# A decoder layer's down projection: order of the weight sums, place of the spare load buffers, and ten split places in the second half

## The chip, the cores and the metric

The kernel runs on one core of a Trainium2 chip. The metric is the device time of one execution in microseconds (us), the median of several runs. A core has five engines with one instruction queue each: PE (matrix products), DVE and POOL (elementwise), ACT (elementwise and functions) and SP (here: it issues DMA transfers). PE writes into eight banks of its accumulator memory; the other engines and the DMA work on the on-chip memory of 128 partitions.

## The reference, cut to what matters

The layer is attention and then a gated feed-forward with a causal depthwise convolution; all is float32, for 256 tokens, a width of 2048 and an inner width of 5632. The change lies in the last product of the feed-forward, here called the down projection:

```python
h = rmsnorm(x, pre_ffn_g)
u = causal_dwconv(h @ w_up, conv_w, conv_b)          # (256, 11264)
gate, val = jnp.split(u, 2, axis=-1)
y = (gelu(gate) * val) @ w_down                      # (256, 5632) @ (5632, 2048)
out = x + rmsnorm(y, post_ffn_g)
```

## The kernel before, in words

**Splitting.** Each float32 operand of a product is split into a high part (ACT copies it into a rounded format, line 333) and a low part (DVE subtracts the high part from the original, line 334); both are in `split` (L332). A product is then three matmuls: high by high, high by low, low by high (`product`, L989).

**Two halves.** The inner width is worked through in two halves (`half`, L1075). Each half computes 11 groups of 256 inner channels with `proj_T4`, `conv` and the gate, and keeps them, split, in the tiles `G` (22 of them) and `sums`. Then come two column passes over `w_down` (n = 0 and n = 2, L1181), each for 1024 of the 2048 output columns. A group is one unit `u` of a pass: two blocks of 128 rows of `w_down`, 1024 columns wide.

**Plain and fast units.** `FAST` holds the units 0, 2, 4, 5, 6 and 7. The other five are plain: two loads, two splits, and eight products (two blocks, two halves of the tokens, two halves of the columns). A fast unit is a 2x2 block product done with seven products (a Winograd scheme): `token_sums` has made the sums of the token side, and the weight side needs three loads. `b11` is 512 columns of the first block. `r13` (1024 columns) is a difference that was formed in DRAM before (`pair_sums`). `r2` (1024 columns) is the second block. `f13` and `b2` are the splits of `r13` and `r2`. Two additions on DVE (L1019 and L1020) then form two more sums, in place in `r2`'s buffer, and `f24` is their split. The seven products take b11 once and each of b2, f13 and f24 twice, in the order of `steps` (L1034). The first fast unit of a pass has an order of its own (L1039).

**The order of units** (L1177 to L1179). Pass n = 0, in both halves: 1, 3, 0, 2, 4, 8, 5, 6, 7, 9, 10. Pass n = 2: 0, 2, 1, 4, 5, 3, 6, 7, 8, 9, 10 in the first half, and 0, 2, 4, 1, 5, 6, 7, 3, 8, 9, 10 in the second. The last unit of a pass is held back (its weights are split but not used at once), and its products are done bank by bank at the end (`block`, L1066), so that each bank can be read out while the next is finished. In the second pass of the second half the last three units are held (`HOLD` is 3): six split forms, which each of the four last blocks reads.

**Load buffers.** `load` (L1132) takes the next of a cycle of buffers of 512 KB: five of the tile `raw`, then `extra`, then two in the room that the convolution's outputs had (`spare`, tag `gates`), and in the second half two more in the room of `hT` (`more`), the input of the up projection. So the cycle has 8 buffers in the first half and 10 in the second. The transfer is issued on SP.

**Split places.** `parts` (L1141) takes the next of a cycle of 6 places for a high and a low part: five of the tiles `whi` and `wlo`, and one pair, `slots`, in the room that the convolution's inputs had (tag `room`). A place is free again when the last product that reads it is done. Each pass makes 34 splits (two per plain unit, four per fast one) and 28 loads (two and three); a half makes 68 and 56.

**Order on the engines.** On PE the program order is kept. On the other engines a planner with a cost model of its own orders the instructions when the kernel is built: an instruction is placed when the planner takes it to be ready, the earlier in the program first. From L1222 on, the order of ACT, DVE, POOL and SP is also that of the program.

**The end** (L1222 to L1262). `x_back` (the residual) and `gbf` (the gain `post_ffn_g`, copied to all partitions, 1 MB) are loaded on SP. `gbf` is a tile with the tag `hT`, so it lies in the first 2048 columns of `hT`'s room. POOL multiplies finished parts of `y` with `gbf` (`gain`, L1196); in its queue the order is `gain` four times, the power that gives the first 128 tokens' factor (`rstd_y`, L1211), `gain` four more times, the power for the other tokens, and a last `gain`. DVE adds the last blocks to `y` (`down`, L1117) and does the final step (`finish`, L1217); the two `finish` steps of the first tokens stand in its queue ahead of `down` of the third block. SP and ACT send the results out.

Of the kernel before, what the change touches and what calls it, by code (L numbers as in the profile page):

```python
# [8 lines left out]
F32 = mybir.dt.float32  # L9
F32R = mybir.dt.float32r  # L10
BF16 = mybir.dt.bfloat16
AF = mybir.ActivationFunctionType
ALU = mybir.AluOpType
# [4 lines left out]
P = 128  # L18
# [14 lines left out]
def hybrid_layer(ctx: ExitStack, tc: tile.TileContext, x, pre_mix_g, w_in, b_forget, sinks,  # L33
# [3 lines left out]
    pe, act, dve, pool, sp = nc.tensor, nc.scalar, nc.vector, nc.gpsimd, nc.sync  # L37
    xf, of = x[0], out[0]
# [4 lines left out]
    main = ctx.enter_context(tc.tile_pool(name="main", bufs=1))  # L43
# [6 lines left out]
    def bank(tag="acc"):  # L50
        return ps.tile([P, 512], F32, tag=tag, bufs=4, name="bank_" + tag)
# [13 lines left out]
    UNIT = 1024  # L65
# [32 lines left out]
    def w_parts(n, keep=None, still=False):  # L98


        if keep and keep[0] is None:
            return keep[1]
        if keep:
            return [keep[0].tile([P, UNIT], F32R, tag="h" + x, bufs=keep[1], name="w" + x)[:, :n]
                    for x in ("hi", "lo")]
        hi = wp.tile([P, UNIT], F32R, tag="whi", bufs=WB, name="whi")
        lo = wp.tile([P, UNIT + 128], F32R, tag="wlo", bufs=WB, name="wlo")
        c = LOW if still else 0
        return [hi[:, :n], lo[:, c:c + n]]
# [31 lines left out]
    def w_unit(src, a, c, keep=None):  # L141
        return w_split(w_load(src, a, c), keep=keep)

    def w_rows(w, k0, a, c0, c):
        return w[k0 * P:(k0 + a) * P, c0:c0 + c].rearrange("(a p) c -> p a c", p=P)
# [61 lines left out]
    hT = main.tile([P, KT, 512], F32R, tag="hT", name="hT")  # L207
# [124 lines left out]
    def split(hi, lo, src):  # L332
        act.copy(hi, src)  # L333
        dve.tensor_tensor(lo, src, hi.bitcast(F32), op=ALU.subtract)  # L334

    with tc.tile_pool(name="mixp", bufs=1) as mp:
# [54 lines left out]
        for u in range(4):  # L391
            if u:
                parts = w_split(first[0][u], True, still=True)
            else:
                parts = w_split(first[0][u], True, begun=begun,
                                between=lambda: x_part(0, (1,), "acc"))
# [5 lines left out]
            parts = w_split(first[1][u], True, still=True)  # L402
# [238 lines left out]
        for g in range(4):  # L641
            if g == 0:
                b2 = bq0
            else:
                b2 = [bank(), bank()]
# [6 lines left out]
        for p0, npair, cols in ((0, 3, 384), (3, 3, 384), (6, 2, 272)):  # L652
            b2 = [bank(), bank()]
            c0 = 3328 + p0 * P
            per = 3 if cols == 272 else 2
            for k0 in range(0, KT, per):
                na = min(per, KT - k0)
                hi, lo = w_unit(w_rows(w_in, k0, na, c0, cols), na, cols)
# [106 lines left out]
        hT = hT2  # L765
# [56 lines left out]
        for n in (2, 3):  # L822
            for u in range(4):
                raw = w_load(w_rows(w_out, 8 + u * 2, 2, n * 512, 512), 2, 512)
# [22 lines left out]
        turns = [turn(0, 0), turn(0, 1)]  # L847
# [8 lines left out]
        turns = [turn(0, 2), turn(0, 3)]  # L856
# [11 lines left out]
    with tc.tile_pool(name="ffn", bufs=1) as fp:  # L868
# [120 lines left out]
        def product(b, lh, ll, rhs, cols, first, last, to=None):  # L989
            hi, lo = rhs  # L990
            for i, (a, r) in enumerate(((lh, hi), (lh, lo), (ll, hi))):
                pe.matmul(b[:, to] if to else b, a, r[:, cols], start=(first and i == 0),  # L992
                          stop=(last and i == 2))

        def column_pass(G, sums, weights, some, order, k00, c0, load, parts, hold=1):

            left, right = slice(0, 512), slice(512, UNIT)
            fast = [u for u in order if u in some]
            plain = [u for u in order[:-hold] if u not in some]
            ready, started, held, banks = {}, set(), [], []  # L1000

            def of(k, t):
                return G[k][:, t * P:(t + 1) * P], G[k][:, 256 + t * P:256 + (t + 1) * P]

            def first(bk):
                new = id(bk) not in started
                started.add(id(bk))
                return new

            def prepare(u):  # L1010
                k = k00 + 2 * u
                if u not in some:
                    return [parts(load(w_rows(w_down, k + a, 1, c0, UNIT)), UNIT)
                            for a in range(2)]
                b11 = parts(load(w_rows(w_down, k, 1, c0, 512)), 512)
                r13 = load(weights[u][:, c0:c0 + UNIT].rearrange("p (a c) -> p a c", a=1))
                r2 = load(w_rows(w_down, k + 1, 1, c0, UNIT))
                f13, b2 = parts(r13, UNIT), parts(r2, UNIT)
                dve.tensor_tensor(r2[:, right], r2[:, right], r13[:, left], op=ALU.add)  # L1019
                dve.tensor_tensor(r2[:, left], r2[:, left], r2[:, right], op=ALU.add)  # L1020
                return b11, b2, f13, parts(r2, UNIT)

            def ahead():
                ready[order[0]] = prepare(order[0])

            def seven(u, forms, m1, m5, m7, m6, p2, p3, p4):
                k, end = 2 * u, u == fast[-1]
                b11, b2, f13, f24 = forms

                def s_of(j):  # L1030
                    return of(k, 1) if j == 3 else [sums[u][:, i * 384 + j * P:i * 384 + (j + 1) * P]
                                                    for i in range(2)]

                steps = [(m1, of(k, 0), b11, left), (p2, of(k + 1, 0), b2, left),  # L1034
                         (p3, s_of(2), b2, right), (m5, s_of(3), f13, left),
                         (m7, s_of(0), f13, right), (m6, s_of(1), f24, right),
                         (p4, of(k + 1, 1), f24, left)]
                if u == fast[0]:
                    steps = steps[0:1] + steps[3:] + steps[1:3]  # L1039
                for bk, a, b, cols in steps:  # L1040
                    product(bk, *a, b, cols, first(bk), end and bk in (m1, m5, m7, m6))

            def run(add_early):
                early, late = ([bank(tag) for _ in range(4)] for tag in ("acc", "att"))
                banks.extend(zip(late, (0, 0, 1, 1), (left, right, left, right)))
                for i, u in enumerate(order):
                    forms = ready.pop(u) if u in ready else prepare(u)
                    if u in some:
                        seven(u, forms, *early, *late[:3])
                        if u == fast[-1] and hold == 1:  # L1050
                            nxt = order[i + 1]
                            ready[nxt] = prepare(nxt)
                            add_early(*early)
                    elif i >= len(order) - hold:
                        held.extend((2 * u + a, forms[a]) for a in range(2))
                    else:
                        for a in range(2):
                            for bk, t, cols in banks:
                                product(bk, *of(2 * u + a, t), forms[a], cols, first(bk),
                                        hold > 1 and bk is late[3] and a == 1 and  # L1060
                                        u == plain[-1])
                if hold > 1:
                    add_early(*early)
                return late

            def block(i, bk=None, cols=None):  # L1066
                b, t, c = banks[i]
                for n, (k, w) in enumerate(held):
                    product(bk or b, *of(k, t), w, cols or c, bk is not None and n == 0,
                            n == len(held) - 1, cols and slice(cols.start - 512, cols.stop - 512))  # L1070

            return ahead, run, block

        ysq = [small.tile([P, 5], F32, tag=f"ysq{t}", bufs=1, name=f"ysq{t}") for t in range(2)]
        for half in range(2):  # L1075
# [5 lines left out]
            for g in range(FHALF // 2):  # L1081
# [25 lines left out]
                if g in FAST:  # L1107
                    i = FAST.index(g)
# [13 lines left out]

            slots = fp.tile([P, ROOM], F32R, tag="room", name="slots")
            slots = [slots[:, 32 + i * UNIT:32 + (i + 1) * UNIT] for i in range(2)]
            spare = fp.tile([P, 2, UNIT], F32, tag="gates", name="spare")
            raws, units = [fp.tile([P, UNIT], F32, tag="extra", name="extra")], [0, 0]
            raws += [spare[:, i, :] for i in range(2)]
            if half:
                more = main.tile([P, 2, UNIT], F32, tag="hT", name="more")
                raws += [more[:, i, :] for i in range(2)]  # L1130

            def load(src):  # L1132
                i = units[0] % (5 + len(raws)) - 5
                units[0] += 1
                c = src.shape[-1]
                if i < 0:
                    return w_load(src, 1, c)[0]
                sp.dma_start(raws[i][:, :c].rearrange("p (a c) -> p a c", a=1), src)
                return raws[i]

            def parts(src, n):  # L1141
                i = units[1] % 6 - 5
                units[1] += 1
                hi, lo = w_parts(n) if i < 0 else [x[:, :n] for x in slots]
                split(hi, lo, src[:, :n])
                return hi, lo

# [33 lines left out]
            for n, (_, run, block) in zip((0, 2), passes):  # L1181
# [6 lines left out]
                for i in range(4):  # L1188
                    block(i)
                    t, c = divmod(i, 2)  # L1190
# [48 lines left out]
        r = rstd_y(0, 3, v)  # L1239
# [18 lines left out]
        r = rstd_y(1, 4, v)  # L1258
        gain(1, 3, 1, last)
        for i, n in enumerate((512, 512, 512, 256, 256)):  # L1260
            c = (0, 512, 1024, 1536, 1792)[i]
# [30 lines left out]
```

## Time and profile before

| | |
|---|---|
| median of 3 runs | 1097.34 us (1096.88 to 1098.96) |
| the profiled execution's own time | 1100.12 us |
| its span, from first to last instruction | 1098.4 us |
| PE busy | 1062.6 us, 97% of the span |
| DVE busy | 855.5 us, 78% |
| ACT busy | 648.6 us, 59% |
| mean granted clock of PE | 0.983 |

The two passes of the first half begin at 581.5 us of the span, those of the second half at 953.1 us. A row of a timeline gives start and duration in us, engine, line, operation, what is written from what, the shape, the number of instructions in it, and in brackets how long the engine had been idle and what released it. In the name of a tile the buffer's number is left out. `SPq` is SP's issue of a transfer. A matmul's duration in a row includes its way through the array; in a row of back-to-back matmuls one starts every 0.23 us. "PEclk" is the clock that PE was granted, 1.00 being full speed.

### The profile page before, as it was taken

Reading aid. Unit: us, or ns where it says so; the run is one execution under the profiler, and the core shown is the slowest. Engines: PE = TensorE matmul, PEld = TensorE weight load, DVE = VectorE, ACT = ScalarE, POOL = GpSimd, SP = SyncE. Lnnn points to the kernel's source line nnn. Section 1 sums busy time; section 2 is a strip of 40 time slices with the busy share of each in tenths; the row PEclk is TensorE's granted clock in tenths of the full one; section 3 lists DMA queues with packets and bytes.
Section 4 is the critical chain, followed back from the end, with each engine's and each line's share of the span. In section 5 each row is a group of like instructions: output and inputs, shape, how many; then the busy total and the mean of one; then the engine's idle time right before and its main releaser. Section 6 shows DMA issues by size and latency. Waiting matters only on the chain.

```text
span 1098.4 us, 16433 instructions
## 1 busy us (share of the span) xinstructions
PE 1062.6 (97%) x5866; PEld 916.9 (83%) x5866; DVE 855.5 (78%) x1389; ACT 648.6 (59%) x1116; POOL 249.4 (23%) x280
## 2 busy tenths in 40 slices
PE   9999999999999999999998989999999999988986
PEld 7899988888889888888886768888888888866765
DVE  5988878876478888878875888867878887768985
ACT  6776757766466765656563545555556565545551
POOL 3254244440032231313130000012222222100013
PEclk9999999999999999999998989999999999989988
DMA  8748688765985987878775657778786866647562
GB/s 277 242 130 238 180 235 243 196 201 168 321 248 174 308 258 224 228 229 235 223 209 163 218 184 245 253 205 239 216 251 211 221 192 198 205 161 261 164 257 77
DMA packets 170798, 238.56 MB, mean 217 GB/s; under 512 B 7996, under 2 KB 132188, under 8 KB 169692
## 3 DMA queue, kind: packets, MB, share of 16 engines
q1 hardware_dynamic: 163184, 222.25, 62.9%
q0 software_dynamic: 6528, 12.58, 7.8%
q10 hardware_dynamic: 1004, 2.68, 0.6%
q8 instruction: 46, 0.75, 0.3%
q14 instruction: 36, 0.29, 0.1%
HBM read 233.14 MB, written 29.38 MB: 239 GB/s over the span
## 4 chain that ended last, share of the span: by engine, by line
PE 76%; DVE 11%; DMA 4%; issue 4%; ACT 4%; POOL 1%; DVEq 0%; SPq 0%; POOLq 0%; ACTq 0%
PE bank_acc L305 15%; PE bank_att L305 13%; PE bank_acc L330 9%; PE bank_acc L311 8%; PE bank_att L311 7%; PE bank_acc L274 7%; PE bank_att L992 7%; DVE wlo L334 4%; PE bank_acc L279 4%; PE bank_acc L992 2%; DVE slots L334 2%; ACT whi L333 1%; DMA spare<-in_w_down_dram 1%; DMA raw<-in_w_out_dram 1%; PE bank_att L496 1%
## 5 line engine op out<-in xcount | busy, mean ns | idle before, releaser
L136 DVE TENSOR_TENSOR wlo<-raw,whi 128x1024 fp32r<-128x1024 f32 (+3 forms) x271 | 332.8, 1241 | 110.5 <-ACT whi L133 102.8
L133 ACT CAST whi<-raw 128x1024 fp32r<-128x1024 f32 (+3 forms) x270 | 273.1, 1029 | 115.1 <-issue 63.4
L922 POOL TENSOR_TENSOR room<-room,rowf 128x256 f32<-128x256 f32 x88 | 100.4, 1160 | 367.5 <-DVE room L921 366.4
L305 PE MATMUL bank_acc<-hT,whi 128*128 128x512 f32 x736 | 173.3, 390 | 0.0
L305 PEld LDWEIGHTS bank_acc<-hT,whi 128*128 128x128 f32 x736 | 136.4, 188 | 27.4
L305 PE MATMUL bank_att<-hT,whi 128*128 128x512 f32 x640 | 150.6, 390 | 0.0
L305 PEld LDWEIGHTS bank_att<-hT,whi 128*128 128x128 f32 x640 | 118.7, 188 | 23.9
L992 PE MATMUL bank_att<-whi,G 128*128 128x512 f32 x342 | 117.6, 404 | 0.0
L924 ACT ACTIVATE room<-room,cw 128x256 f32<-128x256 f32 x88 | 53.0, 602 | 68.5 <-POOL room L922 68.5
L333 ACT CAST whi<-raw 128x1024 fp32r<-128x1024 f32 (+1 forms) x69 | 65.1, 973 | 46.2 <-DVE raw L1020 24.1
L334 DVE TENSOR_TENSOR wlo<-raw,whi 128x1024 fp32r<-128x1024 f32 (+1 forms) x69 | 76.7, 1139 | 19.7 <-ACT whi L333 19.7
L311 PEld LDWEIGHTS bank_acc<-hT,wlo 128*128 128x128 f32 x736 | 89.3, 188 | 2.0
L311 PE MATMUL bank_acc<-hT,wlo 128*128 128x256 f32 x736 | 89.9, 279 | 0.0
L274 PE MATMUL bank_acc<-hT,whi 128*128 128x512 f32 x352 | 88.0, 395 | 0.0
L330 PE MATMUL bank_acc<-whi,oT 128*128 128x512 f32 (+1 forms) x272 | 81.7, 379 | 0.0
L992 PEld LDWEIGHTS bank_att<-whi,G 128*128 128x128 f32 x342 | 67.6, 198 | 14.8
L311 PEld LDWEIGHTS bank_att<-hT,wlo 128*128 128x128 f32 x640 | 77.6, 188 | 1.7
L311 PE MATMUL bank_att<-hT,wlo 128*128 128x256 f32 x640 | 77.9, 279 | 0.0
L926 DVE SCALAR_TENSOR_TENSOR room<-room,cw 128x256 f32<-128x256 f32 x88 | 62.4, 709 | 17.6 <-ACT room L924 17.3
L274 PEld LDWEIGHTS bank_acc<-hT,whi 128*128 128x128 f32 x352 | 63.3, 188 | 11.6
L992 PE MATMUL bank_att<-wlo,G 128*128 128x512 f32 x171 | 69.5, 407 | 0.6 <-DVE wlo L334 0.6
L330 PEld LDWEIGHTS bank_acc<-whi,oT 128*128 128x128 f32 x272 | 50.2, 188 | 9.3
(263 smaller groups left out, 1704.6 us busy)
## 6 DMA issues: line engine op xcount, KB each, us to landing
raw<-in_w_up_dram SPq DMA_DIRECT2D x176, 512.0 KB, 4.6
raw<-in_w_in_dram SPq DMA_DIRECT2D x51, 512.0 KB, 5.6
raw<-in_w_down_dram SPq DMA_DIRECT2D x41, 512.0 KB, 4.8
raw<-in_w_out_dram SPq DMA_DIRECT2D x32, 512.0 KB, 5.8
t<-in_w_down_dram SPq DMA_DIRECT2D x24, 512.0 KB, 6.7
t<-in_w_down_dram POOLq DMA_DIRECT2D x24, 512.0 KB, 8.3
spare<-in_w_down_dram SPq DMA_DIRECT2D x15, 512.0 KB, 5.0
raw<-in_w_in_dram SPq DMA_DIRECT2D x16, 384.0 KB, 3.3
```

The source lines that it names most:

```text
L133: i1 = act.copy(hi[:, cs], raw[:, cs])
L136: i2 = dve.tensor_tensor(lo[:, cs], raw[:, cs], hi[:, cs].bitcast(F32), op=ALU.subtract)
L274: pe.matmul(b, parts[u][0][:, a, m * P:(m + 1) * P], hT[:, kt, :], start=(kt == 0), stop=(kt == KT - 1))
L305: pe.matmul(b, parts[u][0][:, a, m * P:(m + 1) * P], hT[:, kt, :], start=(kt == 0), stop=(kt == KT - 1))
L311: pe.matmul(b[:, 256:512], parts[u][1][:, a, m * P:(m + 1) * P], hT[:, kt, 0:256], start=False, stop=False)
L330: pe.matmul(b, a, r[:, cols], start=(first and i == 0), stop=(last and i == 2))
L333: act.copy(hi, src)
L334: dve.tensor_tensor(lo, src, hi.bitcast(F32), op=ALU.subtract)
L922: pool.tensor_tensor(u[:, 2:258], u[:, 2:258], rowf, op=ALU.mult)
L924: act.activation(y, u[:, 2:258], AF.Identity, bias=cw[:, 3, ch:ch + 1], scale=cw[:, 2, ch:ch + 1])
L926: dve.scalar_tensor_tensor(y, u[:, 1:257], cw[:, 1, ch:ch + 1], y, op0=ALU.mult, op1=ALU.add)
L992: pe.matmul(b[:, to] if to else b, a, r[:, cols], start=(first and i == 0), stop=(last and i == 2))
```

## The change

In `prepare`, the two sums of a fast unit are formed in `r13`'s buffer and not in `r2`'s, and they stand in the program ahead of the split of `r2`: the queue of DVE gets the low part of `f13`, the two sums, the low part of `b2`, the low part of `f24`. Left and right half of `f24` change places with that. In `seven`, the two products of `f13` now stand ahead of the two of `b2`; the first fast unit of a pass keeps its order. In `load`, the cycle has 8 buffers in both halves; the two in the convolution's outputs' room (`spare`) serve for the first time at the 12th and 13th load of a half, not at the 7th and 8th, and the loads 7 to 11 use the five `raw` buffers. In the second half, `hT`'s room holds four more split places instead of two load buffers, so the cycle of split places is 10 long there; it stays 6 long in the first half.

```diff
                 r2 = load(w_rows(w_down, k + 1, 1, c0, UNIT))
-                f13, b2 = parts(r13, UNIT), parts(r2, UNIT)
-                dve.tensor_tensor(r2[:, right], r2[:, right], r13[:, left], op=ALU.add)
-                dve.tensor_tensor(r2[:, left], r2[:, left], r2[:, right], op=ALU.add)
-                return b11, b2, f13, parts(r2, UNIT)
+                f13 = parts(r13, UNIT)
+                dve.tensor_tensor(r13[:, left], r2[:, right], r13[:, left], op=ALU.add)
+                dve.tensor_tensor(r13[:, right], r2[:, left], r13[:, left], op=ALU.add)
+                b2, f24 = (parts(r, UNIT) for r in (r2, r13))
+                return b11, f13, b2, f24
...
-                steps = [(m1, of(k, 0), b11, left), (p2, of(k + 1, 0), b2, left),
-                         (p3, s_of(2), b2, right), (m5, s_of(3), f13, left),
-                         (m7, s_of(0), f13, right), (m6, s_of(1), f24, right),
-                         (p4, of(k + 1, 1), f24, left)]
+                steps = [(m1, of(k, 0), b11, left), (m5, s_of(3), f13, left),
+                         (m7, s_of(0), f13, right), (p2, of(k + 1, 0), b2, left),
+                         (p3, s_of(2), b2, right), (m6, s_of(1), f24, left),
+                         (p4, of(k + 1, 1), f24, right)]
                 if u == fast[0]:
-                    steps = steps[0:1] + steps[3:] + steps[1:3]
+                    steps = steps[0:3] + steps[5:] + steps[3:5]
...
             slots = [slots[:, 32 + i * UNIT:32 + (i + 1) * UNIT] for i in range(2)]
+            if half:
+                more = main.tile([P, 8, UNIT], F32R, tag="hT", name="more")
+                slots += [more[:, i, :] for i in range(8)]
+            extra = fp.tile([P, UNIT], F32, tag="extra", name="extra")
             spare = fp.tile([P, 2, UNIT], F32, tag="gates", name="spare")
-            raws, units = [fp.tile([P, UNIT], F32, tag="extra", name="extra")], [0, 0]
-            raws += [spare[:, i, :] for i in range(2)]
-            if half:
-                more = main.tile([P, 2, UNIT], F32, tag="hT", name="more")
-                raws += [more[:, i, :] for i in range(2)]
+            turn = [None] * 5
+            turns = turn + [extra] + turn
+            turn = [spare[:, 0, :], spare[:, 1, :], extra] + turn
+            units = [0]
 
             def load(src):
-                i = units[0] % (5 + len(raws)) - 5
+                if not turns:
+                    turns.extend(turn)
+                raw, c = turns.pop(0), src.shape[-1]
+                if raw is None:
+                    return w_load(src, 1, c)[0]
+                sp.dma_start(raw[:, :c].rearrange("p (a c) -> p a c", a=1), src)
+                return raw
+
+            def parts(src, n):
+                i = units[0] % (5 + len(slots) // 2) - 5
                 units[0] += 1
...
-                hi, lo = w_parts(n) if i < 0 else [x[:, :n] for x in slots]
+                hi, lo = w_parts(n) if i < 0 else [x[:, :n] for x in slots[i * 2:i * 2 + 2]]
                 split(hi, lo, src[:, :n])
                 return hi, lo
```

More of the change, by code (lines that the diff above doesn't have):

```diff
@@ L1027, in seven @@
                 k, end = 2 * u, u == fast[-1]
-                b11, b2, f13, f24 = forms
+                b11, f13, b2, f24 = forms
                 def s_of(j):
@@ L1124, in hybrid_layer @@
             slots = [slots[:, 32 + i * UNIT:32 + (i + 1) * UNIT] for i in range(2)]
+            if half:
+                more = main.tile([P, 8, UNIT], F32R, tag="hT", name="more")
+                slots += [more[:, i, :] for i in range(8)]
+            extra = fp.tile([P, UNIT], F32, tag="extra", name="extra")
             spare = fp.tile([P, 2, UNIT], F32, tag="gates", name="spare")
-            raws, units = [fp.tile([P, UNIT], F32, tag="extra", name="extra")], [0, 0]
-            raws += [spare[:, i, :] for i in range(2)]
-            if half:
-                more = main.tile([P, 2, UNIT], F32, tag="hT", name="more")
-                raws += [more[:, i, :] for i in range(2)]
-            def load(src):
-                i = units[0] % (5 + len(raws)) - 5
-                units[0] += 1
[L1135 to L1143, printed above, removed]
-                hi, lo = w_parts(n) if i < 0 else [x[:, :n] for x in slots]
+            turn = [None] * 5
+            turns = turn + [extra] + turn
+            turn = [spare[:, 0, :], spare[:, 1, :], extra] + turn
+            units = [0]
+            def load(src):
+                if not turns:
[7 more added lines that the diff above has]
+                i = units[0] % (5 + len(slots) // 2) - 5
+                units[0] += 1
+                hi, lo = w_parts(n) if i < 0 else [x[:, :n] for x in slots[i * 2:i * 2 + 2]]
                 split(hi, lo, src[:, :n])
```

## The prediction, made before the run

> **What bounds the kernel now.** I read the page first, then the chain that ended last, then who waits for whom on PE, then the column passes by windows and timelines. The page:
>
> ```profile
> span 1098.4 us, 16433 instructions
> ## 1 busy us (share of the span) xinstructions
> PE 1062.6 (97%) x5866; PEld 916.9 (83%) x5866; DVE 855.5 (78%) x1389; ACT 648.6 (59%) x1116; POOL 249.4 (23%) x280
> ```
>
> PE sets the pace, and the change leaves its number of matmuls alone. So only time in which PE waits or runs slowly can be won. The change touches the four column passes alone; there the undisturbed pace, the end of the first half and the beginnings are these (chain, then PE's timeline):
>
> ```profile
> 693.82 17.00 PE bank_att L992 x75
> 710.82 3.63 PE bank_acc L305 x16
> ```
> ```profile
> 581.49 0.39 PE L992 MATMUL bank_att<-whi,G 128*128 128x512 f32 x1
> ...
> 953.10 0.39 PE L992 MATMUL bank_att<-whi,G 128*128 128x512 f32 x1
> ...
> 1088.57 0.28 PE L992 MATMUL bank_acc<-whi,G 128*128 128x256 f32 x1
> ```
>
> 17.00 us for 75 matmuls is 0.227 us each. A pass has 6 fast units of 21 matmuls and 5 plain ones of 24, so 246; two passes at that pace take 111.5 us. The first half took 710.8 - 581.5 = 129.3 us, so 17.8 us were lost. The second took from 953.1 to 1088.85, 135.8 us. It has 474 full matmuls and 36 of half the width, 111.6 us, so 24.2 us were lost. Who made PE wait:
>
> ```profile
> PE bank_acc L992 <- ACT whi L333: 7.6, 2, 4.4
> PE bank_acc L992 <- DVE slots L334: 7.4, 6, 1.8
> PE bank_acc L992 <- ACT slots L333: 6.6, 5, 2.1
> ```
>
> That is 21.6 us of the 42, all for split weights. Part of the remainder is clock, which falls around such waits; the four worst windows of 10 us (columns: length, busy time of PE, PEld, DVE, ACT, POOL with counts, PEclk, DMA share, GB/s):
>
> ```profile
> 600.00:610.00 10.00, 8.51 (x27) 6.37 (x27) 8.39 (x10) 5.00 (x6) 0.00 (x0) 0.79 0.56 186
> 640.00:650.00 10.00, 10.00 (x35) 7.93 (x35) 6.41 (x9) 2.10 (x2) 0.00 (x0) 0.74 0.40 147
> 970.00:980.00 10.00, 9.17 (x28) 6.89 (x27) 7.94 (x10) 5.44 (x6) 0.00 (x0) 0.69 0.57 184
> 1060.00:1070.00 10.00, 7.66 (x21) 5.88 (x22) 8.73 (x9) 2.27 (x3) 3.47 (x2) 0.66 0.51 213
> ```
>
> PE busy times one minus the clock gives 1.8, 2.6, 2.8 and 2.6 us.
>
> **Part 1: the buffers of the first loads.** The two waits for ACT whi (7.6 us) are these:
>
> ```profile
> 598.97 0.79 PE L992 MATMUL bank_acc<-whi,sums 128*128 128x512 f32 x1 [4.40 <-ACT whi L333]
> ```
> ```profile
> 969.37 0.80 PE L992 MATMUL bank_acc<-whi,sums 128*128 128x512 f32 x1 [3.19 <-ACT whi L333]
> ```
>
> PE has done unit 0's b11 and f13 and wants f24. Why f24 is late, on SP, ACT and DVE:
>
> ```profile
> 573.38 0.33 SPq L83 DMA_DIRECT2D raw<-t  x1
> ```
> ```profile
> 589.13 0.80 SPq L1138 DMA_DIRECT2D spare<-in_w_down_dram  x2
> ```
> ```profile
> 594.03 1.05 ACT L333 CAST whi<-spare 128x1024 fp32r<-128x1024 f32 x1 [6.22 <-DMA spare<-in_w_down_dram]
> ```
> ```profile
> 587.54 1.23 DVE L334 TENSOR_TENSOR slots<-extra,slots 128x1024 fp32r<-128x1024 f32 x1 [0.38 <-ACT slots L333]
> ```
>
> Unit 0's r2 is the 7th load of the half. Its buffer is `spare`, the convolution's output room, which came free at 589.1 us; it landed at 594.03. With the change it goes into `raw`, whose ring had a free place at 573.38, and lands before f13 is split. Then f13's low part ends at 588.77 as before, the two sums (0.68 each, rows below) end at 590.2, ACT's high part (1.05) at about 591.3 and DVE's low part (1.23) at about 592.6. PE asks for f24 at 598.97 - 4.40 = 594.57: two microseconds of cover, and b2's low part (1.2) may go ahead without using it up. The second half is built alike. I book the whole 7.6 us and the clock of the windows behind both waits, 1.8 + 2.8: together 12.2 us. What is late next is unit 2's f24, in part 2.
>
> **Part 2: the sums ahead of b2's low part, f13's products earlier, ten split places.** The 14.0 us for `slots` are waits for f24 in runs of fast units. Unit 7 in the first half's first pass shows the chain (DVE, then PE):
>
> ```profile
> 630.22 2.35 DVE L334 TENSOR_TENSOR wlo<-spare,whi 128x1024 fp32r<-128x1024 f32 x2
> 632.49 1.22 DVE L334 TENSOR_TENSOR wlo<-raw,whi 128x1024 fp32r<-128x1024 f32 x1
> 633.63 0.68 DVE L1019 TENSOR_TENSOR spare<-spare 128x512 f32<-128x512 f32 x1
> 634.23 1.22 DVE L334 TENSOR_TENSOR wlo<-raw,whi 128x1024 fp32r<-128x1024 f32 x1
> 635.37 0.68 DVE L1020 TENSOR_TENSOR spare<-spare 128x512 f32<-128x512 f32 x1
> 635.97 2.35 DVE L334 TENSOR_TENSOR wlo<-raw,whi 128x1024 fp32r<-128x1024 f32 x2
> 638.24 1.22 DVE L334 TENSOR_TENSOR slots<-spare,slots 128x1024 fp32r<-128x1024 f32 x1
> ```
> ```profile
> 637.18 0.50 PE L992 MATMUL bank_acc<-slots,sums 128*128 128x512 f32 x1 [1.72 <-ACT slots L333]
> ...
> 639.51 1.22 PE L992 MATMUL bank_acc<-slots,sums 128*128 128x512 f32 x2 [1.83 <-DVE slots L334]
> ```
>
> Between the low parts of f13 and b2 (630.22) and that of f24 (638.24) stand four low parts of later units: the planner fills DVE while a sum waits for its predecessor. In the new order the first sum waits for f13's low part alone; b2's serves as a filler itself, so one foreign low part (1.2 us) drops out ahead of the first sum and the wait for b2's high part on ACT (1.05) with it: about 2.2 of the 3.55 us. In the second half four more places let the low parts run ahead in plain units. Against it: b2's place now comes free two products later and r13's buffer is held until f24 is split, while r2's is released earlier. The second half has 8 load buffers, not 10; I price that at nothing, since the first half runs with 8 and loses less (17.8 against 24.2 us). If that cover is gone, a late load costs up to a landing, 4.0 us (row below), once or twice. Of the 14.0 us and the 5.2 us of clock in the other two windows I take two thirds, 12.8 us (2.2 of 3.55, and more where places are ten). Bounds: nothing, and all 19.2 and the short remainder.
>
> The passes together: 12.2 + 12.8 = 25.0 us less; bounds 12 and 33.
>
> **Part 3: what the split places in hT's room delay.** The half makes 68 splits, and the cycle is ten long. Numbered from 0, the six held ones are 62 to 67; 65 goes to the old `slots`, 66 to the first pair in `more`, 67 to the second. The first pair is the room's first 2048 columns, and that is where `gbf` will be loaded. All four last blocks read split 66, the last of them just before PE's final matmul. So the load of `gbf` must wait for the end of PE's work. Today its room was a load buffer, read last by DVE (DVE, SP, DMA issues with KB and us to landing, POOL):
>
> ```profile
> 1057.56 1.22 DVE L334 TENSOR_TENSOR wlo<-more,whi 128x1024 fp32r<-128x1024 f32 x1
> ```
> ```profile
> 1058.81 0.33 SPq L1229 DMA_DIRECT2D gbc_ffn<-in_post_ffn_g_dram  x1
> ```
> ```profile
> gbc_ffn<-in_post_ffn_g_dram SPq DMA_DIRECT2D x1, 1024.0 KB, 7.6
> ...
> more<-t SPq DMA_DIRECT2D x3, 512.0 KB, 4.0
> ```
> ```profile
> 1077.94 2.54 POOL L1199 TENSOR_TENSOR y_sb<-y_sb,gbc_ffn 128x512 f32<-128x512 f32 x2 [7.41 <-ACT junk L1121]
> 1082.28 0.56 POOL L1214 TENSOR_TENSOR ry<-rv,mhalf 128x1 f32<-128x1 f32 x1 [1.80 <-DVE rv L1212]
> ```
>
> The load was issued as soon as that subtraction ended (1058.78), which shows the wait. Behind it on SP stand only result transfers. On POOL the first four gains wait for it, and behind them the power of 1082.28. Behind that wait DVE's two `finish` steps and, in its queue, the last blocks' `down`. PE waits for none of it.
>
> Call PE's end T; it was 1088.85. New: `gbf` issued at T + 0.1; landing 6.0 (between the 4.0 of half a megabyte and the 7.6 with `x_back` in the queue, in the middle because the queue is empty then); four gains of 2.54 / 2 = 1.27, 5.1; the power starts at T + 11.2. From the power to the end of the span it was 1098.4 - 1082.28 = 16.1 us, and I keep that: DVE, POOL and ACT, not PE, carry that stretch. End at T + 27.3. Before: 1098.4 - 1088.85 = T + 9.5. So the tail grows by 17.8 us; bounds by the landing alone 15.8 and 19.4.
>
> The Trainium skill ("DMA: Bandwidth & Descriptors", section "Anatomy of one DMA — SWDGE (gpsimd) path") puts a transfer at about 2.0 us plus its bytes at 436 GB/s, which for this 1 MB would be an estimated 4.4 us. The trace's 7.6 us is far above that, with 2 MB queued ahead; by the page the tail would grow by 16.2 us and not by 17.8.
>
> **The sum.** -25.0 + 17.8 = -7.2 us. The profiled execution, 1100.12 us (span 1098.4), would be 1092.9. The median of 1097.34 lies 2.8 us below that execution, so I forecast 1090.1 for the median, rounded to 1090.
>
> **Rivals.** (a) Only part 1 pays: the planner puts other low parts between the sums as before and f24 stays late. For it: the fillers in the rows at 630 to 638. Against it: the first sum loses a predecessor on two engines. Then -12.2 + 17.8 = +5.6, so 1103. The change turns slower by more than can be told once the passes give less than 15.6 us. (b) The tail does not grow, because `gbf`'s room is not among what the held products read. Against it: the count of splits. Then -25.0: 1072. (c) The passes give about what the tail takes, between 15.6 and 20.0 us: no change. (d) Inside the forecast: all waits and the clock behind them go, 31.4 us: 1084; with the bound of 33 and the smallest tail, 1080.
>
> **How the numbers follow.** About 0.2%, 2.2 us, can be told from no change. The forecast, a gain over 2.2 us with the tail: 0.62. Rival (b): 0.08. Rival (c): 0.12. Rival (a) and what is slower besides: 0.18. So faster 0.70, same 0.12, slower 0.18. The range leaves out (b) and the rare worse cases: 1080 (d) to 1103 (a).
>
> **What would show it.** Right: no wait of PE for ACT near the first fast unit of either half; PE's last matmul near 1064 us (1088.85 - 25); a `gbf` issue right behind it instead of 30 us ahead; four gains back to back with DVE idle; 27 us between PE's end and the span's. Wrong: `gbf` issued before PE's end (the tail), waits for `slots` or `more` as long as today's (part 2), or PE waiting for DMA in the second half (the two buffers less).

## The result, and the profile after

The median went from 1098.03 us (1096.88 to 1098.96, 4 runs) to 1084.50 us (1084.08 to 1084.74, 4 runs): ratio 0.9877, 95% interval 0.986 to 0.9894, so 13.5 us or 1.2% faster. The forecast was 1090, 7 us faster, with a range of 1080 to 1103. The profiled execution of the changed kernel took 1084.41 us, its span is 1082.7 us.

Where the 15.7 us of the two spans (1098.4 and 1082.7) lie is read from the first and the last matmul of each half's passes. The first half took 129.3 us before and 118.6 us after, the second 135.8 and 116.9: the passes gave 10.7 + 18.9 = 29.6 us. From PE's end to the end of the span it was 9.57 us before and 25.75 after: 16.2 us given back. The remaining 2.3 us lie ahead of the passes, in code that didn't change: the first pass began at 581.5 us before and 579.2 after, and in the experiments' profiles anywhere between 579.1 and 582.0.

The 29.6 us in the passes fall into three shares. PE's waits at L992, all rows together, fell from 23.2 to 5.5 us: 17.7. PE's busy time times one minus the granted clock, summed over windows of 10 us as in the prediction, fell from 13.0 to 4.6: some 8. The remaining 3.5 us or so isn't told apart.

Who made PE wait, after (the three rows of before were 21.6 us):

```profile
PE bank_acc L992 <- DVE slots L334: 2.1, 2, 1.6
PE bank_acc L992 <- DVE more L334: 1.4, 1, 1.4
...
PE bank_acc L992 <- ACT slots L333: 1.1, 1, 1.1
...
PE bank_acc L992 <- ACT more L333: 0.7, 1, 0.7
```

The row for ACT `whi` (7.6 us) is gone. What is left is two waits of two steps each, at unit 7 of the first half and at the first f24 of the second, and two short ones of 0.2 and 0.5 us (PE's timeline, idle time in brackets):

```profile
624.42 0.49 PE L992 MATMUL bank_acc<-slots,sums 128*128 128x512 f32 x1 [1.07 <-ACT slots L333]
...
626.55 1.22 PE L992 MATMUL bank_acc<-slots,sums 128*128 128x512 f32 x2 [1.64 <-DVE slots L334]
...
953.78 0.50 PE L992 MATMUL bank_acc<-more,sums 128*128 128x512 f32 x1 [0.68 <-ACT more L333]
...
955.71 0.74 PE L992 MATMUL bank_acc<-more,sums 128*128 128x512 f32 x2 [1.42 <-DVE more L334]
...
1056.08 0.88 PE L992 MATMUL bank_acc<-more,G 128*128 128x256 f32 x6
```

So one sign that the prediction named did not come: near the first fast unit of the second half PE still waits for ACT, 0.68 us, and 1.42 us for DVE behind it. The last row is PE's end, 1056.96 us; its six matmuls read `more`, the split places in hT's room. The end of the kernel on SP, POOL and DVE, and the DMA row of the gain:

```profile
1056.99 0.33 SPq L1233 DMA_DIRECT2D gbc_ffn<-in_post_ffn_g_dram  x1
```
```profile
gbc_ffn<-in_post_ffn_g_dram SPq DMA_DIRECT2D x1, 1024.0 KB, 4.7
```
```profile
1061.78 4.92 POOL L1203 TENSOR_TENSOR y_sb<-y_sb,gbc_ffn 128x512 f32<-128x512 f32 x4 [118.82 <-DMA gbc_ffn<-in_post_ffn_g_dram]
1066.66 0.56 POOL L1218 TENSOR_TENSOR ry<-rv,mhalf 128x1 f32<-128x1 f32 x1
```
```profile
1067.26 3.42 DVE L1222 SCALAR_TENSOR_TENSOR y_sb<-y_sb,ry,x_back 128x512 f32<-128x512 f32 x2 [16.95 <-POOL ry L1218]
```

They are read as one chain. The load is issued 0.03 us after PE's last matmul and lands 4.7 us later; POOL does four gains without a gap, 1.23 us each; the power follows at 1066.66; DVE, idle for 16.95 us, starts its `finish` right behind that. From the power to the end it is 16.0 us, as before (16.1).

### The profile page after: what moved, and what is told of

Read it like the earlier page. It is cut to its first block, busy times and chain, and to the rows that moved or that the text cites. A ratio compares the mean times of both kernels' runs of the same rounds, so it can differ in the third digit from the quotient of the medians.

```text
span 1082.7 us, 16421 instructions
## 1 busy us (share of the span) xinstructions
PE 1048.4 (97%) x5866; PEld 911.0 (84%) x5866; DVE 848.1 (78%) x1389; ACT 648.3 (60%) x1116; POOL 248.2 (23%) x280
## 4 chain that ended last, share of the span: by engine, by line
PE 86%; DVE 7%; issue 3%; ACT 2%; DMA 1%; POOL 1%; SPq 0%; DVEq 0%; POOLq 0%; ACTq 0%
PE bank_acc L305 15%; PE bank_att L305 13%; PE bank_acc L330 12%; PE bank_att L992 10%; PE bank_acc L311 8%; PE bank_att L311 7%; PE bank_acc L274 7%; PE bank_acc L992 4%; PE bank_acc L279 4%; DVE wlo L334 2%; PE bank_att L496 1%; PE bank_att L531 1%; DVE wlo L136 1%; PE bank_acc L955 1%; DVE slots L334 1%
## 5 line engine op out<-in xcount | busy, mean ns | idle before, releaser
L992 PE MATMUL bank_att<-whi,G 128*128 128x512 f32 x298 | 99.4, 394 | 0.0
L333 ACT CAST whi<-raw 128x1024 fp32r<-128x1024 f32 (+1 forms) x61 | 56.6, 957 | 39.3 <-PE bank_att L992 17.5
L334 DVE TENSOR_TENSOR wlo<-raw,whi 128x1024 fp32r<-128x1024 f32 (+1 forms) x61 | 66.5, 1117 | 16.1 <-ACT whi L333 16.1
L992 PEld LDWEIGHTS bank_att<-whi,G 128*128 128x128 f32 x298 | 57.0, 191 | 12.1
L992 PE MATMUL bank_att<-wlo,G 128*128 128x512 f32 x149 | 58.7, 394 | 0.0
```

## The experiments

The theory is that the change wins some 30 us in the passes and gives 16 of them back with the late load. The main rivals: that the end of the kernel is long anyway, and that only one of the parts works. The kernel before was run beside each group; its medians there are 1097.87 (e1, e2, e3, e8), 1098.58 (e4 to e7) and 1097.61 us (e9 to e11).

### The gain's load

**e1: the gain elsewhere.**

```diff
-        gbf = main.tile([P, D], F32, tag="hT", name="gbc_ffn")
+        gbf = fp.tile([P, D], F32, tag="gates", name="gbc_ffn")
```

> The changed kernel, but the gain of the last norm is loaded into the room of the convolution's outputs (the two spare load buffers), which no held product reads. Theory (the load waits for PE's last read of a held split in hT's room, and the first four gains, the power and the last additions wait behind it): the load is issued well before PE's end, about 9.5 us instead of 25.7 pass from PE's end to the end of the span, and the time falls by 16 us, to about 1068. Rival (the end is set by DVE's and POOL's own work, and the late load only fills time that is there anyway): 1084, no change.

Measured: 1066.97 us, ratio 0.9717 (0.9702 to 0.9733). SP, DMA and PE:

```profile
1033.17 0.33 SPq L1233 DMA_DIRECT2D gbc_ffn<-in_post_ffn_g_dram  x1
```
```profile
gbc_ffn<-in_post_ffn_g_dram SPq DMA_DIRECT2D x1, 1024.0 KB, 7.3
```
```profile
1053.52 0.88 PE L992 MATMUL bank_acc<-more,G 128*128 128x256 f32 x6
```

The load is out 21 us ahead of PE's end (1054.40), and the span ends at 1064.0 us, 9.6 us behind it. The theory holds: the room of one 1 MB tile is worth more than the whole measured gain of the change. This version beats both kernels.

**e2: the held splits in other columns.**

```diff
-                slots += [more[:, i, :] for i in range(8)]
+                slots += [more[:, i, :] for i in (4, 5, 6, 7, 0, 1, 2, 3)]
```

> The changed kernel with the four pairs of hT's room in another order, so that the two held splits there lie in columns 4096 to 8191, and the gain's 2048 columns were last used by splits that are long done. Theory A (the wait is for the whole tile, whichever columns it reads): the load is still issued only after PE's last matmul, 1084.5. Theory B (the wait is for the columns that overlap): the load is issued some 20 us ahead of PE's end, and the time is about 1068. I expect A, with a chance of two in three.

Measured: 1083.27 us, ratio 0.9865 (0.9851 to 0.988), 16.3 us above e1.

```profile
1054.93 0.88 PE L992 MATMUL bank_acc<-more,G 128*128 128x256 f32 x6
```
```profile
1055.84 0.33 SPq L1233 DMA_DIRECT2D gbc_ffn<-in_post_ffn_g_dram  x1
```

PE ends at 1055.81, the load goes out at 1055.84, though none of the columns that it writes is still read. A is right: here the tile that takes over the room waits for all readers of the tile before. The prediction argued with the first 2048 columns; it came to the right wait by too narrow a reason.

**e3: the late load by itself.**

```diff
 # in the kernel before
-        gbf = main.tile([P, D], F32, tag="hT", name="gbc_ffn")
+        gbf = fp.tile([P, D], F32, tag="room", name="gbc_ffn")
```

> The kernel before, with one edit: the gain is loaded into the room of the old extra split place, which the fourth held split occupies until the last block. Nothing else of the change. Theory: the price of the late load by itself, 16 us, so 1114; PE's end to the end of the span 25 to 26 us instead of 9.5. Rival (the late load hurt only because the passes had become faster): under 5 us, at most 1103.

Measured: 1113.43 us, ratio 1.0148 (1.0127 to 1.017): 15.6 us for that wait alone, in a kernel whose passes are as slow as before (128.4 and 135.2 us). From PE's end to the end of the span it is 25.0 us.

```profile
1085.31 0.33 SPq L1229 DMA_DIRECT2D gbc_ffn<-in_post_ffn_g_dram  x1
```
```profile
gbc_ffn<-in_post_ffn_g_dram SPq DMA_DIRECT2D x1, 1024.0 KB, 4.6
```

So the price doesn't hang on the faster passes.

### The parts of the change in the passes

| first to last matmul, us | first half | second half | median | less than before |
|---|---|---|---|---|
| before (its own profile) | 129.3 | 135.8 | 1098.03 | |
| e4, load buffers alone | 119.0 | 128.5 | 1081.74 | 16.8 |
| e5, sums and order of products | 123.3 | 128.1 | 1083.99 | 14.6 |
| e6, sums alone | 122.8 | 127.4 | 1083.14 | 15.4 |
| e7, ten places alone | 128.9 | 122.6 | 1090.76 | 7.8 |
| e8, all but the ten places | 117.2 | 122.0 | 1073.92 | 24.0 |
| e1, all, gain elsewhere | 115.8 | 117.0 | 1066.97 | 30.9 |

**e4: the load buffers alone.**

```diff
 # in the kernel before, both halves
-            raws, units = [fp.tile([P, UNIT], F32, tag="extra", name="extra")], [0, 0]
-            raws += [spare[:, i, :] for i in range(2)]
-            if half:
-                more = main.tile([P, 2, UNIT], F32, tag="hT", name="more")
-                raws += [more[:, i, :] for i in range(2)]
+            turn = [None] * 5
+            turns = turn + [extra] + turn
+            turn = [spare[:, 0, :], spare[:, 1, :], extra] + turn
...
# load as in the diff of the change
```

> The kernel before with the new cycle of load buffers alone (eight in both halves, the convolution's room from the 12th load). Theory: PE's two waits for unit 0's f24 (7.6 us) go and with them about 4.6 us of lower clock, while the waits at unit 7 stay as they were: 12 us less, 1085 to 1087. Rival (the waits move to the next f24 in the run of fast units, since DVE has the same work to do): under 6 us less, 1092 or more.

Measured: 1081.74 us, ratio 0.9838 (0.982 to 0.9856). The waits for unit 0's f24 are gone, those for unit 2's behind them too (1.44 us in the first half before, 1.12 in the second), and unit 7's stand as they were:

```profile
627.11 0.50 PE L992 MATMUL bank_acc<-slots,sums 128*128 128x512 f32 x1 [1.77 <-ACT slots L333]
...
629.44 0.73 PE L992 MATMUL bank_acc<-slots,sums 128*128 128x512 f32 x2 [1.83 <-DVE slots L334]
```

The waits did not move on: DVE, which in the kernel before stood idle for 6.01 us until r2 had landed and been split, was now ahead for the whole run of units 0, 2 and 4.

**e5 and e6: the sums, with and without the new order of products.** e5 has both edits of the diff in `prepare` and `seven` in the kernel before. In e6 the products keep their order; only the halves of f24 change places:

```diff
-                         (m7, s_of(0), f13, right), (m6, s_of(1), f24, right),
-                         (p4, of(k + 1, 1), f24, left)]
+                         (m7, s_of(0), f13, right), (m6, s_of(1), f24, left),
+                         (p4, of(k + 1, 1), f24, right)]
```

> The kernel before with the sums ahead of b2's low part and f13's products ahead of b2's, and nothing else. Theory: the waits for unit 0's f24 shrink by about 2 us each (a low part and a high part less in the chain), the waits at unit 7 of about 3.5 us shrink to about 1: together some 8 to 12 us less with the clock, 1086 to 1090. Rival (the planner fills DVE with other low parts as before): no more than 3 us less, 1095.

> As the run with sums and steps, but the seven products keep their old order (b2's products ahead of f13's). Theory (the sums' place on DVE is what counts; the order of the products only moves which split place comes free first): within 2 us of the run with both. Rival (f13's place, freed two products earlier, is what lets the next unit's f13 start and so its f24): at least 4 us slower than the run with both.

Measured: e5 1083.99 us, ratio 0.9862 (0.9846 to 0.9878); e6 1083.14 us, ratio 0.9859 (0.9837 to 0.9881). The order of the products shows no effect (the two are 0.9 us apart, and their runs overlap); the sums carry all of it, and more than the 8 to 12 us expected. e5's unit 0 and unit 7:

```profile
594.31 0.50 PE L992 MATMUL bank_acc<-whi,sums 128*128 128x512 f32 x1 [2.15 <-ACT whi L333]
...
630.31 0.49 PE L992 MATMUL bank_acc<-slots,sums 128*128 128x512 f32 x1 [1.07 <-ACT slots L333]
...
632.44 0.91 PE L992 MATMUL bank_acc<-slots,sums 128*128 128x512 f32 x2 [1.64 <-DVE slots L334]
```

Unit 0's wait falls from 4.40 to 2.15 us, as the theory had it. Unit 7's falls from 1.72 + 1.83 to 1.07 + 1.64, 0.84 us in all, where the prediction took 2.2: a low part does drop out ahead of the first sum, but the planner still puts others ahead of f24's own low part. So unit 7 falls short of the theory, while the kernel gains more than it said.

**e7 and e8: the ten places alone, and all but them.**

```diff
 # e7, in the kernel before, with e1's place for the gain
-                more = main.tile([P, 2, UNIT], F32, tag="hT", name="more")
-                raws += [more[:, i, :] for i in range(2)]
+                more = main.tile([P, 8, UNIT], F32R, tag="hT", name="more")
+                slots += [more[:, i, :] for i in range(8)]
...
-                i = units[1] % 6 - 5
+                i = units[1] % (5 + len(slots) // 2) - 5
...
 # e8, in the changed kernel, which leaves the gain's room free
-            if half:
-                more = main.tile([P, 8, UNIT], F32R, tag="hT", name="more")
-                slots += [more[:, i, :] for i in range(8)]
```

> The kernel before with ten split places in the second half alone: eight load buffers in both halves in the old order, the sums where they were, and the gain loaded into the convolution's outputs' room, so that it isn't late. Theory: the second half's waits in runs of fast units (units 2 and 7) shrink by half, 4 to 8 us with the clock, and the wait for unit 0's f24 stays: 1090 to 1094. Rival (places were not what DVE waited for, since the sums hold the chain up): within 2 us of the kernel before.

> The changed kernel with six split places in both halves: hT's room stays free, so the gain is loaded early, and only the sums, the order of the products and the load buffers differ from the kernel before. Theory: the late load goes (16 us less than the changed kernel), and the second half's passes lose what the four places gave, about 8 us (they would win about 11 us like the first half's, not 19): 1076. Rival (the four places give nothing): 1068. Rival (they give most of the second half's gain): 1084 and more.

Measured: e7 1090.76 us, ratio 0.9924 (0.9904 to 0.9943); e8 1073.92 us, ratio 0.9777 (0.9762 to 0.9792). In e7 the second half's passes take 13.2 us less, more than expected, though unit 0's wait stays and is longer. But the two spare buffers are then read late, and the gain, now in their room, is late again (PE, DVE, SP, DMA):

```profile
971.00 0.79 PE L992 MATMUL bank_acc<-more,sums 128*128 128x512 f32 x1 [4.70 <-ACT more L333]
...
1074.95 0.88 PE L992 MATMUL bank_acc<-more,G 128*128 128x256 f32 x6
```
```profile
1060.97 1.23 DVE L334 TENSOR_TENSOR more<-spare,more 128x1024 fp32r<-128x1024 f32 x1 [0.97 <-ACT more L333]
```
```profile
1062.22 0.33 SPq L1229 DMA_DIRECT2D gbc_ffn<-in_post_ffn_g_dram  x1
```
```profile
gbc_ffn<-in_post_ffn_g_dram SPq DMA_DIRECT2D x1, 1024.0 KB, 5.8
```

The sum of the prediction's part 3, with this issue, gives 1062.2 + 5.8 + 4.9 + 16.1 = 1089.0; the span ended at 1089.3. So even a load 13.6 us ahead of PE's end (1075.83) isn't early enough: from there to the end of the span it is 13.4 us, 3.9 more than before. That the median lies within the 1090 to 1094 expected is luck, since the passes gave more than the theory said and the late gain, which it did not count on, took part of that back.

e8 and e1 differ by the places: 7.0 us in the medians. In the two profiles 5.0 of that lie in the second half's passes, the only ones with more places; the first half's 1.5 us fell in code that is the same. e8 also shows what the places cost: with six there is no wait for unit 0's f24 in the second half, with ten it is 0.70 + 1.43 us (e1).

### Three tries at the rest

**e9** lets the pairs in hT's room join the cycle only from the 13th split on; **e10** changes the first pass's order; **e11** gives e1 the old order of products. All start from e1.

```diff
 # e9
-                i = units[0] % (5 + len(slots) // 2) - 5
+                n0 = units[0]
                 units[0] += 1
+                i = (n0 if n0 < 6 else (n0 - 6) % (5 + len(slots) // 2)) - 5
 # e10
-                       ((0, (1, 3, 0, 2, 4, 8, 5, 6, 7, 9, 10), 1),
+                       ((0, (1, 3, 0, 2, 8, 4, 5, 9, 6, 7, 10), 1),
```

> The first version of this series (the changed kernel with the gain in the convolution's outputs' room, 1066.97 us), and in the second half the four pairs in hT's room join the cycle only from the 13th split on: the first six further splits go round the six old places. Theory (with ten places at once the planner puts unit 2's low parts and sums ahead of unit 0's f24 on DVE, and PE waits 0.70 + 1.43 us there, with a lower clock behind it): that wait shrinks to some 0.2 us as in the run with six places, 3 us less, 1064. Rival (the wait moves on to unit 2 or 4): 1067.

> The same first version, with the first pass of both halves in the order 1, 3, 0, 2, 8, 4, 5, 9, 6, 7, 10: never more than two fast units behind one another. Theory (the remaining wait of the first half at unit 7, 1.19 + 1.47 us, is DVE's backlog of three fast units in a row, each with 5.7 us of DVE work against 4.8 us of PE's): it goes, 3 us less, 1064. Rival (the wait is there because the planner fills DVE with the next plain unit's low parts, so it comes at every fast unit ahead of a plain one): no gain, 1067 to 1070.

> The same first version with the seven products in their old order (b2's ahead of f13's). Theory (the order of the products moves no more than which place comes free first; alone it showed no difference): within 2 us of 1067. Rival (with ten places and the early loads the order decides how far f13 can run ahead): 3 us or more slower, 1070.

Measured: e9 1070.23 us, ratio 0.9736 (0.9716 to 0.9757); e10 1072.43 us, ratio 0.9766 (0.9747 to 0.9785); e11 1067.89 us, ratio 0.9725 (0.9709 to 0.9741). Neither e9 nor e10 gains; e9's runs, 1066.35 to 1070.89, overlap with e1's, 1065.64 to 1068.94. e9's wait at the start went, and a longer one came at unit 2's f24:

```profile
962.24 0.49 PE L992 MATMUL bank_acc<-slots,sums 128*128 128x512 f32 x1 [2.47 <-ACT slots L333]
```

In e10 unit 7's wait went, and two came at units 0 and 2 of the second pass:

```profile
640.47 0.49 PE L992 MATMUL bank_acc<-whi,sums 128*128 128x512 f32 x1 [0.74 <-ACT whi L333]
...
650.04 0.51 PE L992 MATMUL bank_acc<-slots,sums 128*128 128x512 f32 x1 [2.08 <-ACT slots L333]
```

In both the wait that the theory named went, which fits the cause that it gave, but the gain didn't come. e9's rival, that the wait moves to unit 2 or 4, is what happened, at a time 3 us above its 1067. e10's rival put waits at every fast unit ahead of a plain one and the time at 1067 to 1070; of the two new waits only unit 2's stands there, and the time is longer. e11 shows once more no effect of the order of the products. What would remove the last waits stays open. For the one at the start of the second half, e1's DVE queue shows what stands in the way:

```profile
946.03 1.22 DVE L334 TENSOR_TENSOR slots<-extra,slots 128x1024 fp32r<-128x1024 f32 x1
947.16 0.68 DVE L1019 TENSOR_TENSOR raw<-raw 128x512 f32<-128x512 f32 x1
947.77 0.68 DVE L1019 TENSOR_TENSOR extra<-raw,extra 128x512 f32<-128x512 f32 x1
948.37 0.68 DVE L1020 TENSOR_TENSOR raw<-raw 128x512 f32<-128x512 f32 x1
948.97 0.68 DVE L1020 TENSOR_TENSOR extra<-raw,extra 128x512 f32<-128x512 f32 x1
949.57 2.35 DVE L334 TENSOR_TENSOR wlo<-raw,whi 128x1024 fp32r<-128x1024 f32 x2
951.84 1.21 DVE L334 TENSOR_TENSOR more<-extra,more 128x1024 fp32r<-128x1024 f32 x1
```

Unit 0's sums are those on `extra`. Ahead of each of them the planner has put one of unit 2's sums (on `raw`), and ahead of unit 0's f24 (the last row) two other low parts: with more places there is more that is ready to be put in between.

## Why the prediction was right, and where it was off

**Direction and mechanism** were right: faster, by what the passes give less what the late load takes. The terms that were off are the sizes of parts 1 and 2: 25.0 us was booked for the passes, and e1 measured 30.9. The price of the tail was 17.8; e3 measured 15.6, e2 against e1 16.3, the profile after 16.2. The spans differ by 15.7 us where 7.2 were forecast: 4.6 of the 8.5 us between them lie in the passes (29.6 and not 25.0), 1.6 in the tail, and 2.3 ahead of the passes, in code that didn't change. That last share is chance.

**Part 1** (12.2 us) measured 16.8 us alone (e4). There the two waits went as booked; with the ten places a shorter one came back in the second half (0.68 + 1.42 us), which the prediction had not seen. The prediction named unit 2's f24 as what would be late next; e4 shows that it isn't, because DVE no longer starts late. Between the two profiles PE's waits at L992 fell by 11.0 us (23.2 to 12.2) and not by 7.6: besides the two booked, 2.6 us at unit 2 and 0.9 for the low part of unit 0's f24. The remaining 1 us or so of the missing 4.6 is clock and small gaps, and isn't separated.

**Part 2** (12.8 us): the sums alone measured 15.4 us (e6; 14.6 with the new order of products, e5), the places alone 7.8 us, with a late gain (e7); on top of part 1 the sums and the places together give 30.9 - 16.8 = 14.1. The parts overlap, since the loads and the sums both shorten unit 0's wait. Within it the prediction's reading of unit 7 was too kind (0.84 us and not 2.2), and to the second half's places it gave no size of their own: between e8 and e1 they are worth 7.0 us in the medians and 5.0 in the passes. The new order of products counts for nothing (e6, e11). Booking nothing for the two load buffers less has nothing against it: in the second half of the changed kernel PE waits for no DMA, and ACT's waits for loads come to 2.5 us in all, 1.0 at the longest, where a single one before took 5.0. But no run changes the number of buffers alone.

**Part 3** was the step that decided the size, and it was right in each link: issue behind PE's last matmul, four gains in a row, the power, 16 us from there. Only the landing was off, 4.7 us and not 6.0. The sentence on the Trainium skill ("DMA: Bandwidth & Descriptors", section "Anatomy of one DMA — SWDGE (gpsimd) path") gave an estimated 4.4 us and a tail of 16.2; the trace is nearer to it than to the middle between two rows that I took, though the section is about transfers issued by GpSimd and this one was issued on SP. The row of 7.6 us had `x_back` queued ahead of it: in that time the DMA moved 2.6 MB (348 GB/s), and after PE's end this 1 MB alone (210 GB/s over 5 us). e7's 5.8 us, with 1 MB alone as well, shows that this is not all of it.

**Rivals.** (a), slower because only part 1 pays, fails twice: part 2 pays, and part 1 alone would have about paid for the tail (16.8 against 15.6 to 17.5). (b), no tail, fails in the profile; e1 shows that its time, 1072, would have been 1067. (d), all named waits go, is closest in size: 31.4 us booked there, 30.9 measured, and its 1084 is the time that came. That is luck: 5.3 us of the named rows remain, and the 42 us of lost time held more than those rows and the four windows.

## What to carry to other kernels

Before a free room is given to new buffers, look up who takes it over next and when that tile's load must be out: here 1 MB that had been loaded 30 us early went out behind PE's last matmul, and one line moved it away for another 1.5% (e2 against e1). Count a wait with all that goes with it: the passes gained some 30 us where the named waits fell by 16 (21.6 to 5.3); some 8 more were the lower clock, and the rest smaller waits and time that isn't told apart. And where a planner fills an engine's queue, taking one predecessor from a sum may shorten a wait by less than it looks (0.84 us at unit 7 where 2.2 were booked), and a wait removed by hand may come back elsewhere (e9, e10).

## What the runs showed of the hardware

The same two waits cost different amounts in three profiles. At unit 7 of the first half the changed kernel waited 1.07 + 1.64 us, e1 1.19 + 1.47. The windows around and behind it (columns as in the prediction's windows; the granted clock stands behind POOL's busy time), the changed kernel's and then e1's:

```profile
620.00:630.00 10.00, 7.29 (x24) 5.42 (x23) 9.53 (x11) 5.79 (x8) 0.00 (x0) 0.79 0.81 274
630.00:640.00 10.00, 10.00 (x40) 8.08 (x40) 7.18 (x9) 2.24 (x3) 0.00 (x0) 0.87 0.44 173
```
```profile
620.00:630.00 10.00, 7.33 (x31) 5.53 (x31) 10.00 (x12) 6.27 (x8) 0.00 (x0) 1.00 0.79 265
630.00:640.00 10.00, 10.00 (x46) 8.29 (x45) 8.34 (x12) 3.62 (x4) 0.00 (x0) 1.00 0.66 237
```

The clock fell in one and not in the other, and the first half's passes took 118.6 and 115.8 us. PE busy times one minus the clock gives 1.5 + 1.3 = 2.8 us for the first two rows, which is the whole difference. e2, with the same code in the first half and waits of 1.06 + 1.65 us there, lies between: 117.3 us. Windows of 1 us show the steps: after, the clock is 0.50 in all windows from 626 to 632 us and 1.00 again from 633; in e2 it is 0.50 from 627 to 630 only, and 0.84 and 0.95 in the windows beside; in e1 it never falls there. So it was halved for no time in e1, for 3.4 us in e2 and for some 6.8 us after. The Trainium skill ("TensorE: Matmul & The Clock Gate", section "What's actually happening") says that the activity window, about 3.4 us, runs free of the kernel. That fits stretches of about one and two times 3.4 us behind the same two waits; what decides between none, one and two no run here shows.

The load of the gain, 1 MB, landed 4.6 to 4.7 us after its issue, with no other load on the way and PE done or nearly so (after, e2, e3). In e7, also with no other load but with PE and DVE at work, it took 5.8 us; why is open. Where other loads were on the way and the DMA moved 2.6 to 3.8 MB in the same time, it took 7.3 us (e1), 7.6 (before), 10.4 (e4) and 11.2 (e8).
